# A two-layer encoder on one core: softmax divided on ScalarE, layer norms ended in halves, and a smaller DMA scratch traded for four buffers

## Chip, core and metric

The kernel runs on one core of a Trainium2 chip. The metric is the time of one execution on the device in microseconds (us), the median of the runs shown. Engines are named as in the profile: PE (TensorE's matmuls), PEld (its weight loads), DVE (VectorE), ACT (ScalarE), POOL (GpSimd) and SP (SyncE, which only issues DMAs).

## The reference

The input x has 512 tokens of 1024 numbers, the memory 256 tokens. Two layers follow each other, each with four blocks that end in a layer norm:

```python
for i in range(DEPTH):                                   # DEPTH = 2
    y = swiglu(x, ffn_w_gate[i, 0], ffn_w_up[i, 0], ffn_w_down[i, 0])
    x = layer_norm(ALPHA * x + 0.5 * y, ln_g[i, 0], ln_b[i, 0])
    if i % 2 == 0:
        y = mixer_ab(x, ...)      # 8 heads of dense attention, 8 heads within a window of 128
    else:
        y = mixer_c(x, ...)       # 16 heads, each token sees its neighbours on a grid
    x = layer_norm(ALPHA * x + y, ln_g[i, 1], ln_b[i, 1])
    y = memory_attn(x, mem, ...)  # 4 heads into the 256 memory tokens
    x = layer_norm(ALPHA * x + y, ln_g[i, 2], ln_b[i, 2])
    y = swiglu(x, ffn_w_gate[i, 1], ffn_w_up[i, 1], ffn_w_down[i, 1])
    x = layer_norm(ALPHA * x + 0.5 * y, ln_g[i, 3], ln_b[i, 3])
```

`layer_norm` is `(x - mu) * rsqrt(var + eps) * g + b` over the 1024 numbers of a token. Each attention takes a softmax, `exp(s - m) / sum(exp(s - m))`, over the scores of a query.

## The kernel before

All is in float32, and products keep nearly all its digits: `split` (line 360) writes each operand as a high part, rounded on ACT, and a low part, the difference taken on DVE, and `mm3` multiplies three times. So every weight and every intermediate result passes ACT and DVE on its way to PE. The residual x stays in SBUF as four blocks of 128 tokens, `x[t]`; `xh` and `xl` are its two parts with the features on the partitions, made by transposes on PE (`to_features`). The steps of a layer stand in `run`: FFN, mixer, memory attention, FFN.

**Softmax.** In all four attentions a block of queries has its scores in a PSUM bank. DVE takes the extreme score, ACT the exponential and its sum `l` over the row, DVE the reciprocal of `l`, and then `normalise` multiplies the row by it, in place, in an SBUF tile of the tag "t2" (shown as `t` in the profile, as `t_643` and the like in an order). After that PE transposes the row, ACT and DVE split the transposed bank, and PE multiplies with the values. `normalise` chooses the engine by an argument: DVE for the first block of four in dense attention, for blocks 0 and 3 in the neighbourhood attention (whose row it writes as pieces of 64), and for the first of each pair in memory attention; POOL for all others, and for all of windowed attention. In all there are 160 such multiplications: 32 of 512 columns (dense), 16 of 384 and 16 of 256 (windowed), 32 of 192 and 32 of 256 (neighbourhood), 32 of 256 (memory). Dense and windowed attention keep two heads ahead of the one that is being transposed.

**Layer norm.** `layer_norm(t, ...)` follows the last product of block t: DVE makes `nmu` (minus the mean) and `(x + nmu) * g` into a slab, ACT the sum of squares (tile `junk`), POOL the inverse root (`lny`) in two small instructions, and DVE writes `x[t]` with one last instruction of 1024 columns. Only the very last block of the kernel does that in two halves, with an output DMA behind each. `to_features` then transposes the block eight times, four of them from each half of the columns.

**Memory.** SBUF tiles rotate: 27 of the tag "slab" (4 KB per partition) and 14 of "t2" (2 KB per partition). A scratch at the bottom of SBUF, left at its default size, serves the DMAs that POOL issues (line 1628 makes the program). Those are the additions of weight quarters onto slabs by DMA, the gains and offsets of the norms, the additions of x, and the bias tables.

**Order.** No instruction goes out where it is written. `Graph.record` (line 136) notes each with a price in ns by `cost`, `plan` (line 179) lays all of them out on five engines, one instruction at a time, with the buffers as they come free, `deadlines` gives each a due time, and a second plan by due times fixes the order of every engine. The kernel then issues in that order. The price takes in that DVE and POOL can hold each other up: an instruction whose `op.port` is set waits in the plan for the other engine's last one that has it. Since every call goes out from line 154, groups in the profile are told apart by their tiles.

Of the kernel before, what the change touches and what calls it, by code (L numbers as in the profile page):

```python
# [65 lines left out]
class Graph:  # L66
# [69 lines left out]
    def record(self, engine, method, args, kw):  # L136
        kw = dict(kw)
        aps = [z for z in list(args) + list(kw.values()) if hasattr(z, "tensor")]
        outs = [kw[k] for k in ("out", "accum_out") if k in kw]
        if "out" not in kw:  # L140
            outs.insert(0, args[0])
        ins = [z for z in aps if not any(z is o for o in outs)]
        op = Op()
        op.engine, op.index, op.dma, op.adds = engine, len(self.ops), method == "dma_start", "accum_op" in kw
        op.rank = op.index
        op.ns = self.cost(engine, method, outs[0], ins, kw)
        func = args[2] if method == "activation" else None
        op.table = str(func) if func in (AF.Silu, AF.Exp) else None
        op.size = math.prod(outs[0].shape) * 4
        op.port = method in ("tensor_tensor", "scalar_tensor_tensor", "tensor_scalar") and (  # L150
            engine == "gpsimd" or engine == "vector" and op.ns > 250.0 and all(z.space != bass.MemoryType.PSUM for z in ins)
        )
        fn = getattr(getattr(self.nc, engine), method)
        op.call = lambda: fn(*args, **kw)  # L154
        op.deps, op.users, op.frees, op.later = set(), [], [], []
        if self.after and engine in self.after[1]:
            op.deps.add(self.after[0])
        for z, writes in [(z, False) for z in ins] + [(z, True) for z in outs]:
            info = self.tiles.get(z.tensor.name)
            if info is None:  # L160
                continue
            p0, p1, runs = self.extent(z)
            opens = writes and kw.get("start", False)
            keep = []
            for q, w, a0, a1, other in info["log"]:
                over = opens or p0 < a1 and a0 < p1 and (
                    info["bank"] and q.engine != engine or any(l < b and a < h for l, h in runs for a, b in other)
                )
# [148 lines left out]
class Kernel:  # L317
# [16 lines left out]
        return f"{s}_{self.n}"  # L334


    BUFS = {"t2": 14, "slab": 27, "raw": 2, "a": 3, "d": 2, "t": 3}

    def tile(self, pool, shape, dt, tag, bufs=None):
        return self.nc.tile(pool, shape, dt, tag, self.name(tag), bufs or self.BUFS.get(tag, 1))  # L340
# [134 lines left out]
    def layer_norm(self, t, st, gb, last):  # L475

        nc = self.nc
        g, b = gb[:2]
        x = self.x[t]
        halves = [(0, 512), (512, D)] if last and t == NT - 1 else [(0, D)]  # L480
        nmu = self.small(1, "nmu", 4)
        nc.vector.tensor_scalar(nmu, st[:, 0:1], st[:, 1:2], -1.0 / D, ALU.add, ALU.mult)
        var = self.small(1, "var", 4)
        if len(gb) < 3:
            gb.append([])
        if len(gb[2]) < 2:
            gb[2].append(self.slab(F32))
        y = gb[2][t % 2]
        nc.vector.scalar_tensor_tensor(out=y, in0=x, scalar=nmu, in1=g, op0=ALU.add, op1=ALU.mult)
        nc.scalar.activation(self.junk, x, AF.Square, bias=nmu, scale=1.0, accum_out=var)  # L490
        r = self.rsqrt(var, 1, "ln", 1.0 / D, LN_EPS / ALPHA**2)
        for lo, hi in halves:
            nc.vector.scalar_tensor_tensor(
                out=x[:, lo:hi], in0=y[:, lo:hi], scalar=r, in1=b[:, lo:hi], op0=ALU.mult, op1=ALU.add
            )
            if last:
                dst = self.out.rearrange("(r c) d -> c r d", c=GRID_W)[16 * t : 16 * t + 16, :, lo:hi]
                nc.sync.dma_start(out=dst, in_=x[:, lo:hi])
# [421 lines left out]
        self.split(ps[:, lo:hi], h[:, lo:hi], l[:, lo:hi], scale)  # L920
        return h, l

    def normalise(self, u, r, on_vector):
        if not on_vector:
            self.nc.gpsimd.tensor_tensor(out=u, in0=u, in1=r.broadcast_to(list(u.shape)), op=ALU.mult)
        elif u.shape[1] % 192 == 0:

            self.nc.vector.tensor_scalar(u.rearrange("p (z n) -> p z n", n=64), u, r, None, ALU.mult)
        else:
            self.nc.vector.tensor_scalar(u, u, r, None, ALU.mult)  # L930

    def softmax(self, u, rows, mn, lo, n, sums=None, on_vector=False):

        nc = self.nc
        l = self.small(1, "l")
        nc.scalar.activation(u[:rows, :n], sums if sums is not None else u[:rows, :n], AF.Exp, bias=mn[:rows], scale=-1.0, accum_out=l[:rows])
        nc.vector.reciprocal(l[:rows], l[:rows])
        self.normalise(u[:rows, lo:n], l[:rows], on_vector)


    def rope(self, src, n_heads, tab, t, dst):
# [42 lines left out]
    def mixer_ab(self, ln_i, last):  # L984
        nc, a = self.nc, self.a
# [81 lines left out]
        for cg, t in ((1, 0), (1, 1), (1, 2), (0, 0), (1, 3), (0, 1), (0, 2), (0, 3)):  # L1067
            ps = proj(self.ps("a"), t, w1 if cg else w0)
# [16 lines left out]
        def weights_a(pr, s):  # L1085

            p, q = {}, made[False, pr]
            for t in range(NT):
                ps = scores(q[s], kA[s], t, 0, S)
                mn = self.small(1, "mn")  # L1090
                nc.vector.tensor_reduce(out=mn, in_=ps, axis=AX.X, op=ALU.min)
                u = self.t2(F32)
                self.softmax(u, P, mn, 0, S, sums=ps, on_vector=t == 0)
                for kk in range(NT):
                    p[t, kk] = u[:, kk * P : (kk + 1) * P]
            return p
# [73 lines left out]
        for n in range(8):  # L1170
            h, t = divmod(n, 4)
# [8 lines left out]
        for n, (f, v, pr, s) in enumerate(heads):  # L1180
# [39 lines left out]
    def mixer_c(self, ln_i, last):  # L1220
        nc, a = self.nc, self.a
# [74 lines left out]
        def weights_of(pair):  # L1296

            got = []
            for q, k, table in zip(qs.pop(pair), ks.pop(pair), biases(pair)):
# [3 lines left out]
                l = self.small(4, "l4")  # L1303
                us = []
                for t, (kc, w, kind) in enumerate(C_BLOCKS):
                    n = w * ROWS
# [12 lines left out]
                    us.append(u)  # L1319
                nc.vector.reciprocal(l, l)  # L1320
                for t, u in enumerate(us):
                    self.normalise(u, l[:, t : t + 1], t in (0, 3))
                got.append([z[:, c * 256 : c * 256 + 256] for z in both for c in range(2)])
            return got

# [84 lines left out]
    def memory(self, i, ln_i, last):  # L1410
# [36 lines left out]
        def weights_of(kt, q):  # L1447
            p = []
            for tt in range(2):
# [13 lines left out]
                u = self.t2(F32)  # L1463
                for j in range(2):
                    c = slice(j * 256, j * 256 + 256)
                    self.softmax(u[:, c], P, mn[:, j : j + 1], 0, 256, sums=ps[:, c], on_vector=j == 0)
                p.append(u)
            return p

# [165 lines left out]
```

## Time and profile before

| | |
|---|---|
| median of 3 runs | 2139.68 us (2139.59 to 2140.12) |
| the profiled execution's own time | 2138.68 us |
| its span in the profile | 2136.9 us |
| granted clock of PE, mean | 0.998 |
| PE busy | 2114.8 us of the span |
| DVE, ACT, POOL busy | 1764.7, 1081.7 and 379.9 us |

The two attentions of the first mixer lie between 392 and 530 us of the span, dense before 463 and windowed after it; the neighbourhood attention lies between about 1400 and 1620 us. PE's busy time is the union of its matmuls, which overlap, so short waits don't show in it; the idle times of PEld, with what ended them, show more of these. A mean duration is that of one instruction from its start to its end; on one engine, the end of one can lie behind the start of the next.

### The profile page before, as it was taken

Reading aid. Unit: us, or ns where it says so; the run is one execution under the profiler, and the core shown is the slowest. Engines: PE = TensorE matmul, PEld = TensorE weight load, DVE = VectorE, ACT = ScalarE, POOL = GpSimd, SP = SyncE. Lnnn points to the kernel's source line nnn. Section 1 sums busy time; section 2 is a strip of 40 time slices with the busy share of each in tenths; the row PEclk is TensorE's granted clock in tenths of the full one; section 3 lists DMA queues with packets and bytes.
Section 4 is the critical chain, followed back from the end, with each engine's and each line's share of the span. In section 5 each row is a group of like instructions: output and inputs, shape, how many; then the busy total and the mean of one; then the engine's idle time right before and its main releaser. Section 6 shows DMA issues by size and latency. Waiting matters only on the chain.

```text
span 2136.9 us, 33147 instructions
## 1 busy us (share of the span) xinstructions
PE 2114.8 (99%) x12904; PEld 1885.1 (88%) x12904; DVE 1764.7 (83%) x2501; ACT 1081.7 (51%) x1703; POOL 379.9 (18%) x483
## 2 busy tenths in 40 slices
PE   9999999999999999999999999999999999999997
PEld 7999988778888899999889999888888888999996
DVE  7789988898748969999879999876677479699996
ACT  5555543576435544545545455445554355444552
POOL 0001015544002100000200000414420021000003
PEclk9999999999999999999999999999999999999999
DMA  6566562003443246655445556355454432456551
GB/s 206 144 160 147 138 186 88 20 21 97 141 138 99 89 109 188 158 148 138 136 101 130 141 137 180 90 158 147 134 153 156 139 97 91 109 148 157 140 147 60
DMA packets 208717, 275.95 MB, mean 129 GB/s; under 512 B 10673, under 2 KB 151601, under 8 KB 208561
## 3 DMA queue, kind: packets, MB, share of 16 engines
q1 hardware_dynamic: 175760, 221.14, 33.1%
q0 software_dynamic: 32512, 52.44, 13.7%
q8 instruction: 102, 1.67, 0.3%
q14 instruction: 55, 0.44, 0.1%
q10 hardware_dynamic: 288, 0.26, 0.0%
HBM read 259.12 MB, written 4.19 MB: 123 GB/s over the span
## 4 chain that ended last, share of the span: by engine, by line
PE 95%; DVE 3%; ACT 1%; issue 1%; DMA 0%; POOL 0%; POOLq 0%; DVEq 0%; SPq 0%; ACTq 0%
PE a L154 58%; PE d L154 22%; PE t L154 15%; DVE slab L154 1%; DVE x L154 1%; ACT slab L154 1%; DVE t L154 0%; ACT t L154 0%; DMA slab<-t 0%; DMA raw<-x_t 0%; DVE mn L154 0%; POOL t L154 0%; DVE xl L154 0%; POOLq L1631 0%; ACT xh L154 0%
## 5 line engine op out<-in xcount | busy, mean ns | idle before, releaser
L154 DVE TENSOR_TENSOR slab<-slab,slab 128x1024 fp32r<-128x1024 f32 (+3 forms) x638 | 729.3, 1168 | 72.6 <-ACT slab L154 33.1
L154 ACT CAST slab<-slab 128x1024 fp32r<-128x1024 f32 (+2 forms) x498 | 472.4, 983 | 338.6 <-DVE slab L154 139.0
L154 PE MATMUL a<-slab,slab 128*128 128x256 f32 (+2 forms) x2456 | 566.3, 314 | 0.8 <-ACT t L154 0.5
L154 PE MATMUL a<-xh,slab 128*128 128x256 f32 (+2 forms) x2480 | 559.5, 315 | 0.3 <-ACT slab L154 0.3
L154 PE MATMUL d<-slab,slab 128*128 128x512 f32 (+2 forms) x1856 | 449.7, 382 | 2.3 <-DVE x L154 1.8
L154 PEld LDWEIGHTS a<-slab,slab 128*128 128x128 f32 x2456 | 416.5, 190 | 34.7 <-ACT t L154 3.0
L154 PEld LDWEIGHTS a<-xh,slab 128*128 128x128 f32 x2480 | 416.1, 190 | 33.9 <-ACT slab L154 1.0
L154 PE MATMUL a<-xl,slab 128*128 128x256 f32 (+1 forms) x1240 | 389.7, 314 | 0.0
L154 PE MATMUL a<-raw,slab 128*128 128x256 f32 x2048 | 388.7, 283 | 0.9 <-DVE t L154 0.9
L154 PEld LDWEIGHTS d<-slab,slab 128*128 128x128 f32 x1856 | 328.4, 189 | 61.0 <-DVE x L154 2.9
L154 PEld LDWEIGHTS a<-raw,slab 128*128 128x128 f32 x2048 | 327.8, 192 | 6.1 <-ACT slab L154 1.3
L154 PEld LDWEIGHTS a<-xl,slab 128*128 128x128 f32 x1240 | 236.1, 190 | 18.1
L154 PE MATMUL t<-slab,slab 128*128 128x512 f32 (+1 forms) x864 | 209.2, 383 | 0.0
L154 DVE TENSOR_TENSOR slab<-raw,slab 128x1024 fp32r<-128x1024 f32 (+2 forms) x132 | 163.9, 1255 | 19.2 <-ACT slab L154 19.1
L154 PEld LDWEIGHTS t<-slab,slab 128*128 128x128 f32 x864 | 151.4, 189 | 25.1
L154 ACT CAST slab<-t 128x512 fp32r<-128x512 f32 (+2 forms) x211 | 114.1, 567 | 72.0 <-PE t L154 39.0
L154 DVE TENSOR_TENSOR slab<-t,slab 128x512 fp32r<-128x512 f32 (+2 forms) x211 | 132.2, 646 | 10.0 <-ACT slab L154 9.0
L154 ACT CAST slab<-raw 128x1024 fp32r<-128x1024 f32 (+1 forms) x124 | 123.0, 1022 | 28.3 <-PE a L154 9.0
L154 DVE SCALAR_TENSOR_TENSOR x<-d,x 128x512 f32<-128x512 f32 x168 | 114.9, 686 | 17.7 <-PE d L154 16.9
L154 POOL TENSOR_TENSOR t<-t,l 128x256 f32<-128x256 f32 (+2 forms) x104 | 82.9, 819 | 258.8 <-DVE l L154 257.9
L154 ACT COPY t<-a 128x512 f32<-128x512 f32 x96 | 56.3, 587 | 123.7 <-PE a L154 70.1
L154 POOL DMA_DIRECT2D slab<-ffn_w_down x40 | 47.8, 1194 | 313.1 <-DVE slab L154 294.6
(127 smaller groups left out, 2182.5 us busy)
## 6 DMA issues: line engine op xcount, KB each, us to landing
slab<-ffn_w_gate SPq DMA_DIRECT2D x80, 512.0 KB
slab<-ffn_w_up SPq DMA_DIRECT2D x80, 512.0 KB
slab<-ffn_w_down SPq DMA_DIRECT2D x80, 512.0 KB
slab<-ffn_w_down POOLq DMA_DIRECT2D x40, 512.0 KB, 5.6
raw<-mem_w_kv SPq DMA_DIRECT2D x16, 1024.0 KB
slab<-t SPq DMA_DIRECT2D x96, 128.0 KB
slab<-ffn_w_gate POOLq DMA_DIRECT2D x16, 512.0 KB, 7.7
slab<-ffn_w_up POOLq DMA_DIRECT2D x16, 512.0 KB, 5.8
```

Source lines behind the costliest of these rows:

```text
L154: op.call = lambda: fn(*args, **kw)
```

## The change

It has four parts. `normalise` always runs on ACT, as an activation that copies the row with the reciprocal as its scale. `layer_norm` ends in two instructions of 512 columns for blocks 2 and 3 of every norm (for block 2 of the last norm with two output DMAs in place of one). The program is made with 4096 bytes of DMA scratch, and there are 29 slabs and 16 t2 tiles in place of 27 and 14. And in the prices, `op.port` of a DVE instruction asks for 64 columns or more in place of a price over 250 ns.

```diff
-            engine == "gpsimd" or engine == "vector" and op.ns > 250.0 and all(z.space != bass.MemoryType.PSUM for z in ins)
+            engine == "gpsimd" or engine == "vector" and math.prod(outs[0].shape[1:]) >= 64 and all(z.space != bass.MemoryType.PSUM for z in ins)
...
-    BUFS = {"t2": 14, "slab": 27, "raw": 2, "a": 3, "d": 2, "t": 3}
+    BUFS = {"t2": 16, "slab": 29, "raw": 2, "a": 3, "d": 2, "t": 3}
...
-        halves = [(0, 512), (512, D)] if last and t == NT - 1 else [(0, D)]
+        halves = [(0, 512), (512, D)] if t > 1 else [(0, D)]
...
-    def normalise(self, u, r, on_vector):
-        if not on_vector:
-            self.nc.gpsimd.tensor_tensor(out=u, in0=u, in1=r.broadcast_to(list(u.shape)), op=ALU.mult)
-        elif u.shape[1] % 192 == 0:
-
-            self.nc.vector.tensor_scalar(u.rearrange("p (z n) -> p z n", n=64), u, r, None, ALU.mult)
-        else:
-            self.nc.vector.tensor_scalar(u, u, r, None, ALU.mult)
-
-    def softmax(self, u, rows, mn, lo, n, sums=None, on_vector=False):
+    def normalise(self, u, r):
+        self.nc.scalar.activation(u, u, AF.Copy, scale=r)
+
+    def softmax(self, u, rows, mn, lo, n, sums=None):
...
-        self.normalise(u[:rows, lo:n], l[:rows], on_vector)
+        self.normalise(u[:rows, lo:n], l[:rows])
...
-    nc = bacc.Bacc("TRN2", target_bir_lowering=False, num_devices=1)
+    nc = bacc.Bacc("TRN2", target_bir_lowering=False, num_devices=1, dynamic_dma_scratch_size=4096)
```

(The three callers of `softmax` and `normalise` drop the argument that chose the engine.)

The plan changes with it. On ACT, this is the start of dense attention before, just behind the load of the exponential's table; rows that write `t` and `l` are exponentials with their sums, those from `t` to `slab` are halves of queries:

```order
L154 ACTIVATE t_643_724,l_725<-a_722,mn_723 128x512
L154 ACTIVATE slab_642<-t_699 64x128
L154 ACTIVATE t_647_728,l_729<-a_726,mn_727 128x512
L154 ACTIVATE t_655_736,l_737<-a_734,mn_735 128x512
L154 ACTIVATE slab_642<-t_706 64x128 x2
L154 ACTIVATE slab_751<-t_750 64x512
L154 ACTIVATE t_651_732,l_733<-a_730,mn_731 128x512
L154 ACTIVATE t_659_740,l_741<-a_738,mn_739 128x512
```

And the same place after; rows that read and write one `t` tile, with an `l`, are the divisions:

```order
L154 ACTIVATE t_643_724,l_725<-a_722,mn_723 128x512
L154 ACTIVATE t_639_720<-t_639_720,l_721 128x512
L154 ACTIVATE slab_642<-t_699 64x128
L154 ACTIVATE t_647_728,l_729<-a_726,mn_727 128x512
L154 ACTIVATE t_655_736,l_737<-a_734,mn_735 128x512
L154 ACTIVATE slab_642<-t_706 64x128
L154 ACTIVATE t_643_724<-t_643_724,l_725 128x512
L154 ACTIVATE t_647_728<-t_647_728,l_729 128x512
L154 ACTIVATE slab_642<-t_706 64x128
L154 ACTIVATE t_659_740,l_741<-a_738,mn_739 128x512
L154 ACTIVATE t_651_732,l_733<-a_730,mn_731 128x512
```

The divisions stand between the exponentials, two to six rows behind the one that they belong to; whatever follows a division waits behind it on the same engine.

On DVE, at the norm ahead of the neighbourhood attention, block 2 (`x_6`) before; `st` are the sums for the mean, `xl` the low parts of transposed blocks:

```order
L154 SCALAR_TENSOR_TENSOR slab_2500<-x_6_87,nmu_2521,slab_2493 128x1024
L154 SCALAR_TENSOR_TENSOR x_7_88,st_2526<-d_2527,x_7_88 128x512
L154 SCALAR_TENSOR_TENSOR x_7_88,st_2526<-a_2528,x_7_88 128x512
L154 SCALAR_TENSOR_TENSOR x_6_87<-slab_2500,lny_2523,slab_2494 128x1024
L154 TENSOR_SCALAR nmu_2529<-st_2526 128x1
```

And after:

```order
L154 SCALAR_TENSOR_TENSOR slab_2500<-x_6_87,nmu_2521,slab_2493 128x1024
L154 TENSOR_TENSOR xl_84<-t_2512,xh_83 128x4x128
L154 SCALAR_TENSOR_TENSOR x_7_88,st_2526<-d_2527,x_7_88 128x512
L154 SCALAR_TENSOR_TENSOR x_6_87<-slab_2500,lny_2523,slab_2494 128x512
L154 SCALAR_TENSOR_TENSOR x_7_88,st_2526<-a_2528,x_7_88 128x512
L154 SCALAR_TENSOR_TENSOR x_6_87<-slab_2500,lny_2523,slab_2494 128x512
L154 TENSOR_SCALAR nmu_2529<-st_2526 128x1
```

The first half of block 2 is written one instruction of block 3 earlier, the second half behind that instruction.

On PE, at the same norm, the transposes of block 2 (`ident` and `x_6`) before, between products of the next stage:

```order
L154 MATMUL a_2543<-slab_2539,xh_83 128x256
L154 MATMUL t_2524<-ident_78,x_6_87 128x128 x4
L154 MATMUL t_2525<-ident_78,x_6_87 128x128 x4
L154 MATMUL a_2543<-slab_2540,xh_83 128x256
L154 MATMUL a_2543<-slab_2539,xl_84 128x256
```

And after:

```order
L154 MATMUL a_2543<-slab_2539,xl_84 128x256
L154 MATMUL t_2524<-ident_78,x_6_87 128x128 x4
L154 MATMUL a_2544<-slab_2537,xh_83 128x256
L154 MATMUL a_2544<-slab_2538,xh_83 128x256
L154 MATMUL t_2525<-ident_78,x_6_87 128x128 x4
```

The eight transposes that stood together are two groups of four with two products between them, and the first now stands behind the last product of `a_2543`.

More of the change, by code (lines that the diff above doesn't have):

```diff
@@ L1092, in weights_a @@
                 u = self.t2(F32)
-                self.softmax(u, P, mn, 0, S, sums=ps, on_vector=t == 0)
+                self.softmax(u, P, mn, 0, S, sums=ps)
                 for kk in range(NT):
@@ L1321, in weights_of @@
                 for t, u in enumerate(us):
-                    self.normalise(u, l[:, t : t + 1], t in (0, 3))
+                    self.normalise(u, l[:, t : t + 1])
                 got.append([z[:, c * 256 : c * 256 + 256] for z in both for c in range(2)])
@@ L1465, in weights_of @@
                     c = slice(j * 256, j * 256 + 256)
-                    self.softmax(u[:, c], P, mn[:, j : j + 1], 0, 256, sums=ps[:, c], on_vector=j == 0)
+                    self.softmax(u[:, c], P, mn[:, j : j + 1], 0, 256, sums=ps[:, c])
                 p.append(u)
```

## Prediction

> **What bounds the kernel now.** First the head of the page and of its chain.
>
> ```profile
> span 2136.9 us, 33147 instructions
> PE 2114.8 (99%) x12904; PEld 1885.1 (88%) x12904; DVE 1764.7 (83%) x2501; ACT 1081.7 (51%) x1703; POOL 379.9 (18%) x483
> PE 95%; DVE 3%; ACT 1%; issue 1%; DMA 0%; POOL 0%; POOLq 0%; DVEq 0%; SPq 0%; ACTq 0%
> ```
>
> TensorE is busy 99% and carries 95% of the chain. The change takes no matmul away, so it can only win time in which TensorE waits. That time is small: 2136.9 - 2114.8 = 22.1 us by the busy time, with the start and the end of the program in it. Next the stretches of the mixers: dense attention (A, 392 to 463), windowed attention (B, to 530), neighbourhood attention (C, 1400 to 1620).
>
> ```profile
> core 0: us, PE busy (x) PEld busy (x) DVE busy (x) ACT busy (x) POOL busy (x), PEclk, DMA share, GB/s
> 392.00:463.00 71.00, 68.66 (x360) 54.96 (x358) 65.34 (x141) 47.13 (x112) 36.76 (x41) 1.00 0.06 16
> 463.00:530.00 67.00, 64.76 (x394) 56.84 (x393) 59.85 (x166) 48.37 (x127) 32.90 (x64) 1.00 0.23 64
> 1400.00:1620.00 220.00, 219.81 (x1380) 196.26 (x1380) 155.61 (x332) 115.91 (x260) 66.47 (x122) 1.00 0.54 156
> ```
>
> In A and B together TensorE is busy 133.42 of 138 us, VectorE 125.19 (91%), ScalarE 95.50 (69%). In C TensorE misses 0.2 us of 220, so C has nothing to give. Matmuls overlap and hide short waits in the busy time, so I take the waits of the weight loads, in the stretch of A and B:
>
> ```profile
> PEld t L154 <- DVE slab L154: 4.5, 9, 1.8
> PEld a L154 <- ACT t L154: 3.0, 9, 0.7
> PEld d L154 <- DVE x L154: 1.4, 2, 0.9
> PEld t L154 <- PE a L154: 0.6, 1, 0.6
> PEld d L154 <- ACT slab L154: 0.5, 1, 0.5
> PEld a L154 <- DVE slab L154: 0.5, 1, 0.5
> PEld d L154 <- ACT t L154: 0.4, 1, 0.4
> PEld d L154 <- DVE slab L154: 0.3, 1, 0.3
> ```
>
> Sum 11.2 us, more than a third of the kernel's waits. VectorE ends 4.5 + 1.4 + 0.5 + 0.3 = 6.7 of it (it empties PSUM banks late), ScalarE 3.9. POOL is not in the list: its divisions are waited for only indirectly.
>
> **The change, part by part.**
>
> *The division.* These rows, in order, are the divisions of today (first three POOL, next three VectorE) and ScalarE's nearest operations, with a pointer operand and SBUF on both sides:
>
> ```profile
> L154 POOL TENSOR_TENSOR t<-t,l 128x256 f32<-128x256 f32 x64 | 40.7, 650 | 217.4 <-DVE l L154 217.1
> L154 POOL TENSOR_TENSOR t<-t,l 128x512 f32<-128x512 f32 x24 | 27.5, 1167 | 24.9 <-DVE l L154 24.9
> L154 POOL TENSOR_TENSOR t<-t,l 128x384 f32<-128x384 f32 x16 | 15.5, 974 | 16.5 <-DVE l L154 15.9 <-ACT slab L154 0.5
> L154 DVE TENSOR_SCALAR t<-t,l 128x192 f32<-128x192 f32 x32 | 19.7, 646 | 0.4
> L154 DVE TENSOR_SCALAR t<-t,l 128x512 f32<-128x512 f32 x8 | 10.5, 1312 | 0.0
> L154 DVE TENSOR_SCALAR t<-t,l 128x256 f32<-128x256 f32 x16 | 8.8, 570 | 0.2
> L154 ACT ACTIVATE t<-t,mn 128x385 f32<-128x385 f32 x16 | 9.8, 616 | 4.1 <-DVE mn L154 4.1
> L154 ACT ACTIVATE t<-t,mn 128x257 f32<-128x257 f32 x16 | 8.1, 508 | 0.7 <-POOL t L154 0.3 <-DVE mn L154 0.2
> L154 ACT ACTIVATE t<-t,mn 128x192 f32<-128x192 f32 x32 | 14.2, 445 | 4.6 <-issue 3.8 <-DVE mn L154 0.5
> L154 ACT ACTIVATE junk<-x,nmu 128x1024 bf16<-128x1024 f32 x32 | 36.8, 1151 | 66.6 <-DVE nmu L154 61.9 <-issue 4.7
> ```
>
> 104 divisions leave POOL, 56 VectorE (39.0 us), and 160 come to ScalarE. By these widths a ScalarE division of 512 is between 616 (385 wide) and 1151 (1024 wide): on the line, 722 ns; 384 wide 616, 256 wide 508, 192 wide 445. When operations stand back to back, each takes about 0.1 less:
>
> ```profile
> 333.02 1.07 ACT L154 CAST xh<-t 128x512 fp32r<-128x512 f32 x2 [0.88 <-PE t L154]
> L154 ACT CAST xh<-t 128x512 fp32r<-128x512 f32 x56 | 30.7, 587 | 48.8 <-PE t L154 48.8
> ```
>
> (two of 587 in 1.07 us). A and B have 32 of 512, 16 of 384, 16 of 256: 23.1 + 9.9 + 8.1 = 41.1 us alone, 41.1 - 6.4 = 34.7 back to back. ScalarE then has 95.5 + 34.7 = 130.2 to 136.6 us of work in a stretch that takes 138 and in which TensorE needs 138 - 11.2 = 126.8. VectorE falls by the 10.5 us of its eight 512-wide divisions to 114.7. So the fullest helper changes from VectorE at 91% to ScalarE. By these figures the stretch could shrink by at most 138 - 130.2 = 7.8 us. ScalarE's 95.5 hold many operations that stand alone and would close up, so 130.2 is rather too much.
>
> In its favour: VectorE's division is irregular where POOL works beside it, and the plan that fixes all orders prices it at 399 ns (512 / 1.92 + 132), against 1312 measured.
>
> ```profile
> L154 DVE TENSOR_SCALAR t<-t,l x8: 486/1241/2684, 395.0 to 462.7; 128x512 f32<-128x512 f32 x8
> ```
>
> The same formulas price ScalarE's at 572, some 50 ns under my back-to-back 622. The written order will lie closer to what happens, and the nine waits on "DVE slab" are of the sort that such surprises make. I take 5.0 of the 6.7 us as gone and 1.0 more on ScalarE: **-4.0 us**, between -7.8 and +9 (below). What is late next is ScalarE: exponentials and first halves of the splits stand behind a division that waits for its reciprocal. In C the 64 divisions are 32 x 0.445 + 32 x 0.508 = 30.5 us beside 115.9 of 220; with that room they cost nothing. In memory attention 16 per layer, 8.1 us, lie likewise; 0.
>
> [...]
>
> *The halves.* Two norms are followed by a visible wait of TensorE's transposes, at 341 to 350 us (first row) and at 1390 to 1402 (the next):
>
> ```profile
> PEld t L154 <- issue: 0.9, 1, 0.9
> PEld t L154 <- issue: 1.0, 1, 1.0
> L154 DVE SCALAR_TENSOR_TENSOR x<-slab,lny,slab 128x1024 f32<-128x1024 f32 x31 | 39.6, 1280 | 1.0 <-POOL lny L154 0.9
> L154 DVE SCALAR_TENSOR_TENSOR x<-slab,lny,slab 128x512 f32<-128x512 f32 x2 | 1.4, 747 | 0.4 <-POOL lny L154 0.4
> ```
>
> The first four transposes may go 1280 - 747 = 533 ns earlier: 2 x 0.53 = **-1.1 us**; from 0 to the whole 1.9. Fifteen norms gain an instruction, each 1.4 - 1.28 = 0.12 us, 1.8 us in all on VectorE, mostly beside matmuls. At the very end block 2's two halves keep the last norm's POOL power where it is, or let it in between them (-0.6 to +0.1): 0.
>
> *Buffers, scratch, prices.* The ring of POOL's DMAs shrinks to a quarter.
>
> ```profile
> q0 software_dynamic: 32512, 52.44, 13.7%
> ```
>
> 32512 packets over 112 issues are 290 each, some 18 per engine. No row shows what the ring can hold; what hides a delay is that the added quarters are wanted a whole step of matmuls later. I take 0, between 0 and +6 (each of the 112 late by 50 ns on the path). The four buffers and the new order elsewhere: TensorE already runs without gaps through the FFNs, so at best the stray waits go, such as this at 128 us:
>
> ```profile
> PEld a L154 <- ACT slab L154: 1.3, 1, 1.3
> ```
>
> I take **-0.9**, from -4 to +4, since a new order can also open waits of this size.
>
> Sum: -4.0 - 1.1 - 0.9 = **-6.0 us**. Against the profiled execution (2138.68, its span of 2136.9 and 1.8 around it) that is 2132.7; the median of the runs is 2139.68, 1.0 above it, so I forecast **2133.7**.
>
> **Rivals.**
> 1. *ScalarE becomes the queue of A and B* (slower). Its place is the heads between 392 and 530. If ScalarE can be filled no better than VectorE is today (125.19 of 138, 90.7%), its middle of 133.4 us needs 147: +9, less 2 from the other parts, 2146.7. It decides from where ScalarE's need passes TensorE's 126.8 us, which by its busy time it does. Against it: ScalarE's isolated operations close up, and VectorE and POOL get room.
> 2. *Waits change their name.* As many waits go from "DVE slab" as come on "ACT"; only the halves stay: -1.1, 2138.6. For it: ScalarE ends 3.9 us of the waits already at 69%.
> 3. *The change doesn't do what it says*: the plan shifts waits elsewhere or the small ring delays POOL's DMAs: +6, 2145.7. Against it: the gapless FFNs and the 18 packets.
>
> **Chances.** My forecast, with larger gains, 0.50; the second rival and what lies near it 0.27; the first 0.17; the third 0.06. A measurement of this kernel tells about 0.2% (4.3 us) from no change: faster 0.50, same 0.27, slower 0.23. The range runs from 2125 (7.8 + 1.9 + 4, and about 1 of the rest) to 2145, just short of the first rival's middle, so that about a tenth lies beyond each end.
>
> **What would show it.** Right: waits of the weight loads on "DVE slab" between 390 and 530 fall below 2 us, and that stretch is some 4 us shorter, with ScalarE over 92% busy; the two norms' waits halve. Wrong: rows "PEld t" or "PEld a" ended by ACT sum to over 8 us there (first rival), or to as much as VectorE loses (second); gaps in the FFNs, or "POOL DMA" rows far over their present durations (third). A ScalarE division of 512 well over 722 ns would break the sum.

## The result, and the profile after

The changed kernel takes **2144.69 us** (2142.46 to 2147.01, 11 runs) beside 2140.02 of the kernel before (2138.16 to 2141.77, 11 runs): ratio 1.0022, 95% interval 1.0015 to 1.003. It is slower by 4.7 us, little but clear of 1 by its interval, where 6 us less was forecast.

The head and the chain of waits of the profile after:

```profile
span 2142.3 us, 33001 instructions
PE 2117.1 (99%) x12904; PEld 1885.7 (88%) x12904; DVE 1725.2 (81%) x2460; ACT 1151.2 (54%) x1863; POOL 288.0 (13%) x379
PE 91%; ACT 3%; DMA 3%; DVE 2%; issue 1%; POOL 0%; SPq 0%; DVEq 0%; ACTq 0%
```

VectorE and POOL lost 39.5 and 92 us of work, ScalarE took 69.5 more, as the change says. But TensorE's share of the chain fell from 95 to 91%, and DMA, at 0% before, has 3%. The same three stretches as in the prediction, with their columns:

```profile
core 0: us, PE busy (x) PEld busy (x) DVE busy (x) ACT busy (x) POOL busy (x), PEclk, DMA share, GB/s
392.00:463.00 71.00, 69.48 (x370) 55.90 (x369) 58.21 (x138) 65.36 (x145) 11.57 (x21) 1.00 0.06 16
463.00:530.00 67.00, 66.10 (x393) 57.04 (x391) 56.11 (x161) 61.92 (x159) 5.02 (x27) 1.00 0.26 70
1400.00:1620.00 220.00, 212.97 (x1321) 188.29 (x1320) 127.13 (x289) 136.53 (x319) 34.59 (x86) 0.99 0.55 152
```

In the first two TensorE is busier than before (135.6 of 138 us in place of 133.4). In the third, where it had missed 0.2 us of 220, it now misses 7.0. What it waits for there is in the waits of the weight loads from 1400 to 1625 us; first before, then after (total, times, longest):

```profile
PEld t L154 <- DVE t L154: 1.7, 6, 0.3
PEld a L154 <- DMA slab<-t: 0.4, 1, 0.4
```

```profile
PEld a L154 <- DMA slab<-t: 5.1, 2, 4.5
PEld a L154 <- issue: 2.9, 3, 1.8
PEld t L154 <- DVE t L154: 2.1, 6, 0.4
```

`slab<-t` are the copies that `queries` and `keys` of the neighbourhood attention end with: twelve of 128 KB per pair of heads, four from `queries` and eight from `keys`, issued by SP, from which the scores of a later pair are made. The 4.5 us are one wait, for the eight of the last pair's keys. On the timeline around it (start, duration, and in brackets the idle time and what ended it), before:

```profile
1572.82 4.97 SPq L154 DMA_DIRECT2D slab<-t  x8
1580.65 0.57 POOL L154 DMA_DIRECT2D slab<-ln_g  x1 [12.19 <-DVE mn L154]
1584.13 1.20 POOL L154 TENSOR_TENSOR t<-t,l 128x256 f32<-128x256 f32 x2 [2.92 <-DVE l L154]
...
1586.76 0.59 POOL L154 DMA_DIRECT2D slab<-ln_b  x1
```

and after:

```profile
1572.35 0.56 POOL L154 DMA_DIRECT2D slab<-ln_g  x1 [14.79 <-PE t L154]
1572.91 0.54 POOL L154 DMA_DIRECT2D slab<-ln_b  x1
1573.01 5.41 SPq L154 DMA_DIRECT2D slab<-t  x8
1583.79 0.33 PE L154 MATMUL a<-slab,slab 128*128 128x192 f32 x1 [4.10 <-DMA slab<-t]
1584.56 0.73 PE L154 MATMUL a<-slab,slab 128*128 128x192 f32 x3 [0.45 <-DMA slab<-t]
```

SP issues the copies at nearly the same time in both. The norm's gains and offsets (`ln_g`, `ln_b`, 512 KB each on POOL's queue, which VectorE first needs for the norm at 1610 us) went out 8 and 14 us after the first copy; now they go out just ahead of it. What the queues then move from 1575 to 1578 us (packets, MB, share of the 16 engines), after:

```profile
q0 software_dynamic: 109, 0.42, 91.7%
q1 hardware_dynamic: 3, 0.00, 0.4%
```

and before:

```profile
q1 hardware_dynamic: 403, 0.66, 89.0%
```

q0 is POOL's queue, q1 SP's. For three microseconds POOL's queue holds the engines nearly alone, and the copies, of which five more are issued in these 3 us, stand still. The 0.42 MB are less than the 512 KB of one load, so the first load, of the gains, is enough for that; in the microsecond behind it POOL's queue still has 87.3% and SP's 10.6%.

To compare stages of kernels that run at different times, I count TensorE's waiting at equal points of its work: the start of each matmul, less the sum of the usual pitches of all matmuls ahead of it (0.227 us for 512 columns, 0.120 for 256, the medians in the kernel before). Its growth by stage in us (worked out from the starts of all 12904 matmuls of each profile; the experiments are those below):

| stage | before | after | e3 | e6 | e8 | e9 | e12 |
|---|---|---|---|---|---|---|---|
| to the first mixer | 5.6 | 4.6 | 4.5 | 3.8 | 6.1 | 3.4 | 3.5 |
| dense and windowed attention | 10.9 | 9.2 | 9.3 | 9.1 | 9.4 | 8.3 | 8.2 |
| then to the second mixer's norm | 3.9 | 4.5 | 4.1 | 3.9 | 3.2 | 4.6 | 3.0 |
| that norm | 2.2 | 1.8 | 1.8 | 2.8 | 2.2 | 2.8 | 2.8 |
| neighbourhood attention | 5.6 | 15.3 | 9.3 | 6.4 | 11.3 | 15.9 | 6.7 |
| the rest | 2.5 | 1.6 | 1.6 | 2.8 | 1.5 | 2.0 | 2.1 |
| sum | 30.6 | 37.0 | 30.6 | 28.8 | 33.6 | 36.9 | 26.1 |

One profile is one execution: that of e5, which has the orders of the kernel before on every engine and differs by its scratch alone, sums to 32.2 in place of 30.6, so I read nothing into differences of 1.6 us between two profiles unless runs or several profiles agree.

The changed kernel was 2.5 us ahead when it came to the neighbourhood attention, and lost 9.7 there. By the same count 5.0 of these (4.3 and 0.7) are the wait at 1579 us; a second, of 1.7 and 0.5 us at 1486 us, is also for copies. And right behind the long wait the granted clock of TensorE (the column PEclk) is at half for 3.4 us, and then at full again (columns as above):

```profile
1584.90:1588.30 3.40, 3.40 (x19) 3.40 (x18) 1.87 (x10) 2.19 (x8) 0.00 (x0) 0.50 1.01 363
1588.30:1592.00 3.70, 3.70 (x24) 3.33 (x24) 1.32 (x9) 2.94 (x11) 0.00 (x0) 1.00 0.42 168
```

Half of 3.4 us makes 1.7 us more, as an estimate. That makes 8.9 of the 9.7 us; the rest is spread over the stage. The kernel before has no such stretch until its matmuls are over.

### The profile page after: what moved, and what is told of

It reads as the page before. It is cut to its first block, busy times and chain, and to the rows that moved or that the text cites. A ratio compares the mean times of both kernels' runs of the same rounds, so it can differ in the third digit from the quotient of the medians.

```text
span 2142.3 us, 33001 instructions
## 1 busy us (share of the span) xinstructions
PE 2117.1 (99%) x12904; PEld 1885.7 (88%) x12904; DVE 1725.2 (81%) x2460; ACT 1151.2 (54%) x1863; POOL 288.0 (13%) x379
## 4 chain that ended last, share of the span: by engine, by line
PE 91%; ACT 3%; DMA 3%; DVE 2%; issue 1%; POOL 0%; SPq 0%; DVEq 0%; ACTq 0%
PE a L154 57%; PE d L154 20%; PE t L154 14%; ACT t L154 2%; ACT slab L154 1%; DVE slab L154 1%; DMA slab<-t 1%; DMA slab<-ffn_w_up 1%; DVE t L154 0%; DVE x L154 0%; DMA raw<-ab_w_out 0%; DMA raw<-c_w_in 0%; DMA raw<-x_t 0%; DMA raw<-mem_t 0%; DVE mn L154 0%
## 5 line engine op out<-in xcount | busy, mean ns | idle before, releaser
L154 PE MATMUL a<-slab,xh 128*128 128x512 f32 (+1 forms) x272 | 79.5, 375 | 0.8 <-ACT xh L154 0.7
```

## The experiments

Three theories stood at the start. **Theory 1**: a POOL without divisions issues its loads earlier, and they run into the copies. **Theory 2**: ScalarE's queue delays the parts of the queries and keys. **Theory 3**: the four new buffers free the loads' slabs earlier. Ratios are to the kernel before, on the same chip, with 95% intervals; each profile is of one execution.

### e1: the old divisions, everywhere

The changed kernel, with `normalise` and its callers as before; halves, buffers, scratch and prices stay.

```diff
-    def normalise(self, u, r):
-        self.nc.scalar.activation(u, u, AF.Copy, scale=r)
+    def normalise(self, u, r, on_vector=None):
```

> The changed kernel with the softmax divided on VectorE and POOL as before; halves, price rule, small scratch and the four buffers stay. Theory 1 (freed POOL): the neighbourhood attention lost about 10 us because POOL, rid of its divisions, issues its DMAs (gains and offsets of the norm, bias tables) earlier, into the copies of queries and keys that TensorE waits for; with the divisions back the 10 us go and about 2.5 us of the gain in the first mixer go too: about 2137 us. Theory 2 (ScalarE queue in the neighbourhood attention): the same 2137. Theory 3 (buffers): the slabs of these loads come free earlier because there are 29, so the collision stays: 2145 to 2147 us.

Measured: 2141.67 us, ratio 1.0005 (0.9996 to 1.0013): between the theories. The gains still go out early, at 1572.16 us, but the offsets at 1585.69, behind the last divisions, and the wait is 0.75 us instead of 4.3 and 0.7, with no stretch at half clock. So the gains go early whoever divides; that the offsets follow at once comes from the divisions' leaving POOL.

### e2: the old buffers

The changed kernel with the buffers and the scratch of before.

```diff
-    BUFS = {"t2": 16, "slab": 29, "raw": 2, "a": 3, "d": 2, "t": 3}
+    BUFS = {"t2": 14, "slab": 27, "raw": 2, "a": 3, "d": 2, "t": 3}
-    nc = bacc.Bacc("TRN2", target_bir_lowering=False, num_devices=1, dynamic_dma_scratch_size=4096)
+    nc = bacc.Bacc("TRN2", target_bir_lowering=False, num_devices=1)
```

> The changed kernel with 27 slabs, 14 t2 tiles and the default DMA scratch; divisions on ScalarE, halves and the price rule stay. Theory 1 (freed POOL): the collision stays, some wait of TensorE on the copies of queries of over 3 us near the end of the neighbourhood attention, 2143 to 2147 us. Theory 3 (buffers): it goes, 2138 to 2140 us. Theory 2 (ScalarE queue): stays, but with waits that ScalarE ends.

Measured: 2140.07 us, 0.9998 (0.999 to 1.0007). POOL's rows on the timeline:

```profile
1584.17 0.56 POOL L154 DMA_DIRECT2D slab<-ln_g  x1 [19.88 <-DVE mn L154]
1584.84 0.54 POOL L154 DMA_DIRECT2D slab<-ln_b  x1
```

With 27 slabs POOL waits 12 us longer for a slab, and both loads go out behind the copies; no wait is left at 1579 us. Theories 1 and 3 are each half right: the buffers make the slab free early, and the empty POOL lets the second load follow. Waits of 1.7 and 1.1 us at 1486 to 1490 us stay, here with a stretch at half clock behind them, so these do not hang on the buffers.

### e3: the norm's loads behind the copies

The changed kernel; in `mixer_c` the two loads are issued by SP.

```diff
-    def load_ln(self, i):
+    def load_ln(self, i, queue="gpsimd"):
...
-            self.nc.gpsimd.dma_start(out=z, in_=self.a[name][i : i + 1, :].broadcast_to([P, D]))
+            getattr(self.nc, queue).dma_start(out=z, in_=self.a[name][i : i + 1, :].broadcast_to([P, D]))
...
-        gb = self.load_ln(ln_i)
+        gb = self.load_ln(ln_i, "sync")
```

> The changed kernel, with the two loads of gains and offsets of the norm behind the neighbourhood attention issued by SP in place of POOL; there they stand behind the copies of queries and keys. Theory 1 and theory 3 (a collision of these loads with the copies): the wait of 4.1 us and the 0.5 behind it go, 2144.7 - 4.6 = about 2140 us; the waits at 1486 us (2.2) stay. Theory 2 (ScalarE queue): no change, 2144 to 2145 us.

Measured: 2138.53 us, 0.9992 (0.9983 to 1.0001), against 1.0022 of the changed kernel. The loads now go out behind the copies on the same queue:

```profile
1572.86 5.07 SPq L154 DMA_DIRECT2D slab<-t  x8
1579.82 0.64 PE L154 MATMUL d<-slab,slab 128*128 128x256 f32 x4
1580.02 0.42 SPq L154 DMA_DIRECT2D slab<-ln_g  x1
1580.53 0.59 SPq L154 DMA_DIRECT2D slab<-ln_b  x1
```

TensorE goes on without a wait, and the granted clock stays at 1.00. The part of the stage with this wait falls from 7.3 to 1.1 us, the time by 6.2. Theory 2's "no change" is out for this wait. Only the queue of these two loads was changed (and what the plan made of it), so the wait at 1579 us is shown to be the collision with them.

### e4: the old divisions in the neighbourhood attention alone

The changed kernel; POOL and VectorE divide in the neighbourhood attention as before.

```diff
-                    self.normalise(u, l[:, t : t + 1])
+                    self.normalise(u, l[:, t : t + 1], t in (0, 3))
```

> The changed kernel, with the old division on VectorE and POOL in the neighbourhood attention alone (dense, windowed and memory attention divide on ScalarE). Theories 1 and 2: the gain of the first mixer and the norms (3.8 us up to 770 us) stays and the 10 us of the neighbourhood attention go: 2135 to 2138 us. Theory 3 (buffers): 2142 us or more, since the loads still find a slab early.

Measured: 2138.66 us, 0.9991 (0.9982 to 1.0). Gains at 1571.76 us, offsets at 1585.01, a wait of 0.83 us. The same reading as from the first run, though the time is 0.7 us above the range of theories 1 and 2. It is also 3.0 us below the first run, which differs only in that VectorE and POOL divide in the other attentions too.

### e5: each part alone: the scratch

Here and in e6 to e10 the base is the kernel before.

```diff
-    nc = bacc.Bacc("TRN2", target_bir_lowering=False, num_devices=1)
+    nc = bacc.Bacc("TRN2", target_bir_lowering=False, num_devices=1, dynamic_dma_scratch_size=4096)
```

> The kernel before with nothing but the 4 KB of DMA scratch. Collision theory (the early loads of the last norm's gains and offsets delay the copies of the last pair): the scratch sets no order, so no change, ratio 0.999 to 1.001 (2138 to 2142 us), and the additions of ffn_w_down take 5.5 to 6 us from issue to landing, as before. Rival (the small ring delays POOL's DMAs): 3 us or more slower, 2143 us or above, with longer times from issue to landing.

Measured: 2140.1 us, 1.0004 (0.9995 to 1.0013): no effect that can be told. POOL's additions of `ffn_w_down`, 512 KB each, land 5.7 us after their issue (median of 40), against 5.6 before.

### e6: each part alone: the buffers (with the scratch that pays for them)

```diff
-    BUFS = {"t2": 14, "slab": 27, "raw": 2, "a": 3, "d": 2, "t": 3}
+    BUFS = {"t2": 16, "slab": 29, "raw": 2, "a": 3, "d": 2, "t": 3}
```

> The kernel before with 29 large and 16 small buffers and the 4 KB of scratch; divisions, norms and prices as before. Collision theory in its two-condition form (the load needs an early slab, and the offsets need a POOL free of divisions): the gains go out near 1572 us instead of 1580, the offsets stay behind the four divisions, and the wait near 1579 us is under 1.2 us; 2139 to 2142 us. Rival (the buffers alone cause the loss): a wait of over 4 us near 1579 us and 2143 to 2146 us.

Measured: 2137.21 us, 0.999 (0.9981 to 0.9998): better than either theory had it.

```profile
1568.51 0.58 POOL L154 DMA_DIRECT2D slab<-ln_g  x1 [7.39 <-PE t L154]
1576.26 0.62 PE L154 MATMUL a<-slab,slab 128*128 128x192 f32 x3 [0.41 <-DMA slab<-t]
1581.54 0.60 POOL L154 DMA_DIRECT2D slab<-ln_b  x1
```

The gains are early and TensorE waits 0.4 us, and 0.3 more at 1578 us; the offsets are held back by the divisions at 1580.4. Elsewhere the buffers win: 1.8 us ahead of the first mixer and 1.8 in its two attentions.

### e7: each part alone: the halves

```diff
-        halves = [(0, 512), (512, D)] if last and t == NT - 1 else [(0, D)]
+        halves = [(0, 512), (512, D)] if t > 1 else [(0, D)]
```

> The kernel before with nothing but the halves of the layer norms. If the gain ahead of the first mixer is theirs: TensorE's wait at 341 to 350 us falls from 1.75 to under 0.5, other norms gain up to 0.5 each, the stage of the neighbourhood attention stays at 5 to 6 us of waits; 2136.5 to 2139 us, ratio 0.9985 to 0.9995. Rival (the added instructions on VectorE cost what they win, or the plan shifts other waits in): 2139.5 to 2142 us.

Measured: 2137.98 us, 0.9991 (0.9983 to 1.0), within the expected range, but not by its reasons. The first norm's wait falls from 1.75 to 0.61 us and 1.1 of new waiting comes right behind it; the second norm's stays (2.21, then 2.23); others gain nothing. The profiled execution is only 0.5 us shorter (span 2136.4). What it wins lies at the very end: from the last matmul to the end of the span 11.5 us instead of 12.3.

### e8: each part alone: the divisions

```diff
-    def normalise(self, u, r, on_vector):
+    def normalise(self, u, r):
+        self.nc.scalar.activation(u, u, AF.Copy, scale=r)
```

> The kernel before with nothing but ScalarE's divisions; buffers, scratch, norms and prices as before. Collision theory: without the four buffers the gains go out after 1580 us, no wait of over 1.2 us near 1579, and TensorE's waits in the two first attentions fall from 10.9 to 9 to 10 us; 2138 to 2141 us. Rival (ScalarE's queue costs in the neighbourhood attention whatever the buffers are): waits there rise from 5.5 to over 12 us and the time is 2144 us or more.

Measured: 2141.77 us, 1.0007 (0.9998 to 1.0015), 0.8 above the expected range and 2.2 below the rival's. Waits in the two first attentions are 9.4 us, as expected, and there is none at 1579 us. But the neighbourhood attention rises from 5.6 to 11.3 us of waiting, by waits for copies of 2.0 us at 1487 and others near 1490 and 1536, and by 3.4 us at half clock from 1491.1 us on. The rival asked for over 12, so it nearly holds for the waits: divisions on ScalarE cost in that stage even without the new buffers. By which step, the queue of ScalarE or the new order, this run does not tell.

### e9: buffers and divisions together

Both edits above, with norms and prices as before.

> The kernel before with ScalarE's divisions and with 29 large and 16 small buffers (and the 4 KB of scratch); norms and prices as before. These two alone measured 2137.2 us (buffers) and 2141.8 (divisions) beside 2139.6 of before. Theory of two conditions (the four buffers free the slabs early, the empty POOL lets the offsets follow the gains at once): TensorE waits over 3.5 us near 1579 us, though neither part alone had 1.2 us there, and the time is 2143 to 2147 us. Rival (the parts add up, the long wait hangs on the halves or the prices): no wait over 1.5 us there, 2138 to 2140.5 us.

Measured: 2142.76 us, 1.0014 (1.0005 to 1.0023). The time is 0.2 below the expected range, and the wait is 2.2 and 0.7 us in place of "over 3.5"; the rival's "no wait over 1.5" is out.

```profile
1573.71 0.56 POOL L154 DMA_DIRECT2D slab<-ln_g  x1 [14.79 <-PE t L154]
1574.27 0.54 POOL L154 DMA_DIRECT2D slab<-ln_b  x1
1574.37 5.38 SPq L154 DMA_DIRECT2D slab<-t  x8
1583.24 0.33 PE L154 MATMUL a<-slab,slab 128*128 128x192 f32 x1 [2.20 <-DMA slab<-t]
```

Both loads go out just ahead of the copies, as in the changed kernel. Neither part alone does this; halves and prices aren't needed for it. The wait is shorter than in the changed kernel, but not by a later TensorE: loads, copies and TensorE all come 1.4 us later, after 3.2 us lost at 1485. What differs is that the loads went faster. This is POOL's queue from 1572 to 1585 us (packets, MB, share of the engines), after and in this run:

```profile
q0 software_dynamic: 288, 1.05, 36.7%
```

```profile
q0 software_dynamic: 288, 1.05, 29.4%
```

The offsets landed 8.6 us after their issue instead of 10.6; why, no run shows. The stage loses as much as in the changed kernel all the same (15.9 us), since here the clock is at half for 3.4 us twice, behind the wait at 1485 and behind this one.

### e10: buffers and halves together

The edits of e6 and e7, with divisions and prices as before.

> The kernel before with the four buffers, the scratch and the halves; divisions and prices as before (with the new price rule the same measured 2141.7 us). If these two parts add up: 2135 to 2136.5 us, ratio 0.998 to 0.9985, and the new price rule costs some 5 us by the order that it sets. Rival (the halves and the buffers do not add up, the rule is nothing): 2140 to 2143 us, with the wait of 1.9 us at 1488 us.

Measured: 2139.48 us, 0.9996 (0.9987 to 1.0005), with no wait at 1488 us. The runs fall between the two theories, while the profiled execution (span 2135.3) would fit the first: the runs' median lies 4.2 us above the span here, -0.5 to 3.3 in the other kernels. Whether the two parts add up stays open; the wait at 1488 does not come from them.

### e11: old divisions in the neighbourhood attention and the loads on SP

The edits of e3 and e4 on the changed kernel.

> The changed kernel with the old divisions in the neighbourhood attention alone and, there, the loads of the norm's gains and offsets issued by SP behind the copies. Each of the two alone measured 2138.6 us beside 2140.3 of before. If both act on the one collision: no more than 1.5 us below either, 2137 to 2138.7 us, no wait over 0.6 us near 1579, the wait of 1.7 us at 1488 us stays. Rival (they act on different waits and add up): 2132 to 2135 us.

Measured: 2137.34 us, 0.9989 (0.998 to 0.9998). The long wait is gone, and hardly more is gained than by either edit alone, as expected if both act on the one collision. But 0.7 us of waiting for copies are left at 1582 us, just over the expected 0.6, though the loads go out behind the copies (1581.3 us), and the wait at 1486 us did not stay at 1.7 but grew to 2.6, with a stretch at half clock behind it: TensorE comes 0.4 us earlier than in e4, and the copies that it waits for land 0.5 us later.

### e12: buffers, and divisions outside the neighbourhood attention

The kernel before with 29 slabs, 16 t2 tiles and the scratch, and this; `mixer_c` still calls `normalise` with `t in (0, 3)`.

```diff
-    def normalise(self, u, r, on_vector):
-        if not on_vector:
+    def normalise(self, u, r, on_vector=None):
+        if on_vector is None:
+            self.nc.scalar.activation(u, u, AF.Copy, scale=r)
+        elif not on_vector:
...
-                self.softmax(u, P, mn, 0, S, sums=ps, on_vector=t == 0)
+                self.softmax(u, P, mn, 0, S, sums=ps)
```

> The kernel before with the four buffers and the scratch, and ScalarE's divisions in dense, windowed and memory attention alone; norms, prices and neighbourhood attention as before. If the divisions win in the first two attentions what the waits say (about 1.5 us) and the order elsewhere stays as with the buffers alone: 2135 to 2136.5 us. Rival (the new order shifts waits of 1 to 2 us in, as the new prices did): 2137.5 to 2141 us.

Measured: **2135.42 us**, 0.998 (0.9971 to 0.999): below both kernels. Its three stretches:

```profile
392.00:463.00 71.00, 70.31 (x374) 56.73 (x373) 59.86 (x141) 65.94 (x145) 10.75 (x23) 1.00 0.06 16
463.00:530.00 67.00, 65.48 (x387) 55.97 (x387) 56.18 (x158) 60.32 (x155) 4.63 (x23) 1.00 0.29 79
1400.00:1620.00 220.00, 219.06 (x1359) 194.07 (x1358) 153.36 (x332) 115.36 (x260) 55.52 (x117) 1.00 0.54 152
```

The first two are as full as in the changed kernel (135.8 us), and TensorE misses 0.9 us in the third instead of 7.0. Against the buffers alone (e6) the waiting in the first two falls from 9.1 to 8.2 us, where 1.5 was expected, and the intervals of the two times overlap.

### e13: the second wait: a third load buffer

The wait at 1485 to 1488 us divides the kernels in two. Behind the 1 MB loads of `c_w_in`, SP issues the copies of a pair; the distance from the first of these loads to the first copy, and TensorE's waits for the copies from 1482 to 1494 us, both read from the timelines and waits:

| kernels | distance, us | waits, us |
|---|---|---|
| e6, e10, e12, later e14 | 6.7 to 6.8 | none |
| before, e5, e7 | 5.2 to 5.5 | 0.2 to 0.3 |
| after, e1, e2, e3, e4, e8, e9, e11 | 2.8 to 3.4 | 1.9 to 3.0 |

The changed kernel with one load buffer more and two slabs less.

```diff
-    BUFS = {"t2": 16, "slab": 29, "raw": 2, "a": 3, "d": 2, "t": 3}
+    BUFS = {"t2": 16, "slab": 27, "raw": 3, "a": 3, "d": 2, "t": 3}
```

> The changed kernel with a third load buffer (raw 3 in place of 2) paid for by two slabs (27 in place of 29); all else as changed. If the wait at 1485 to 1488 us comes from the 1 MB loads of c_w_in that go out just ahead of the copies: the loads go out 5 us or more ahead of the copies and the wait falls from 2 us to under 0.6. With 27 slabs the gains of the last norm go out after 1580 us, so the 4.3 us near 1579 go too. Together 2136 to 2139 us. Rival (the copies are late by their own source, whatever goes before): the wait there stays at 1.5 us or more, 2138.5 to 2141 us.

Measured: 2136.38 us, 0.9982 (0.9973 to 0.9991). The long wait is gone, as with any 27 slabs (gains at 1579.46 us). But the loads go out only 2.2 us ahead of the copies, so the third buffer did not do what it was for, and the wait of 1.5 us stays. This run therefore does not tell whether the distance is the cause.

### e14: the second wait: the old prices

The kernel of e4, with the old price rule.

```diff
-            engine == "gpsimd" or engine == "vector" and math.prod(outs[0].shape[1:]) >= 64 and all(z.space != bass.MemoryType.PSUM for z in ins)
+            engine == "gpsimd" or engine == "vector" and op.ns > 250.0 and all(z.space != bass.MemoryType.PSUM for z in ins)
```

> The changed kernel with the old divisions in the neighbourhood attention and the old price rule (so e4_neighbourhood_as_before, which measured 2138.7 us, without the new prices). If the new prices open the wait at 1488 us by the order of the casts of c_w_in: the loads go out over 5 us ahead of the copies, the wait is under 0.6 us, 2135 to 2137 us. Rival (the halves together with the buffers do it): the wait stays at 1.5 us or more and 2138 to 2140 us.

Measured: 2137.35 us, 0.9987 (0.9979 to 0.9996), a little above the expected range. SP's timeline with the new prices (e4), then with the old:

```profile
1476.27 1.51 SPq L154 DMA_DIRECT2D raw<-c_w_in  x2
1479.44 7.86 SPq L154 DMA_DIRECT2D slab<-t  x8
```

```profile
1472.50 3.90 SPq L154 DMA_DIRECT2D raw<-c_w_in  x2
1479.23 5.45 SPq L154 DMA_DIRECT2D slab<-t  x8
```

One line of prices moves the loads by 3.8 us, and the wait goes with it. Some of what that frees is lost at 1577 us, where TensorE now waits 1.8 us for copies behind the early gains, instead of 0.8. In both kernels the gains go out 0.6 us ahead of the first copy, so why the wait is longer stays open; one early load alone is not always cheap. So the new prices open the second wait, and so do ScalarE's divisions in this stage (e8, which has the old prices). That the distance of loads and copies makes the wait fits all sixteen kernels, but no run changed the distance alone.

## Why the prediction was wrong

**The step that failed** is "so C has nothing to give", with the zero for its 64 divisions ("with that room they cost nothing"). The idle 0.2 us said that there was nothing to win; I read it as nothing to lose. The stage lost 9.7 us. ScalarE's room (115.9 of 220 us, now 136.5) was not the limit that matters. What matters is the order in which transfers go out: POOL's divisions were a gate in POOL's queue, which held the 512 KB of offsets back until the copies had landed, and the shortage of slabs was another for the gains. The change opened both. Behind the wait that followed the clock was at half for 3.4 us, a price that no term of the sum had.

**The buffers, scratch and prices, -0.9 from -4 to +4.** The scratch was rightly 0. The buffers alone won 2.1 us by the ratio (e6). What I did not ask is which transfer an earlier free slab would start, and into what. Together with the divisions, that is the wait shown above; e3 prices it at 6.2 us, outside my +4.

**The third rival had the number.** Its 2145.7 us lie 1.0 from the measured time, and its words "the plan shifts waits elsewhere" fit; it had a chance of 0.06. That the number is so near is luck: its +6 was worked out from 112 late DMAs of the small ring. The evidence set against it, the gapless FFNs and the 18 packets, speaks of the small scratch and of another stage. The two loads that matter were not delayed; they were too early.

**Dense and windowed attention, -4.0.** Sign right, size not: the waiting there falls by 1.7 us in the changed kernel, and by 1.5 with the divisions alone. The prices of the step hold. ScalarE's divisions, after:

```profile
L154 ACT ACTIVATE t<-t,l 128x256 f32<-128x256 f32 x80 | 36.2, 503 | 0.9 <-DVE l L154 0.9
L154 ACT ACTIVATE t<-t,l 128x512 f32<-128x512 f32 x32 | 21.6, 735 | 0.0
L154 ACT ACTIVATE t<-t,l 128x192 f32<-128x192 f32 x32 | 14.2, 447 | 1.0 <-DVE l L154 0.9
```

735 ns for 512 columns against 722 estimated; ScalarE has 127.3 of 138 us (92.2%) against "over 92%", VectorE 114.3 against 114.7. What failed is "I take 5.0 of the 6.7 us as gone". The waits of the weight loads from 392 to 530 us, after:

```profile
PEld t L154 <- DVE slab L154: 5.6, 11, 1.0
PEld a L154 <- ACT t L154: 1.7, 5, 0.5
PEld t L154 <- ACT t L154: 0.7, 3, 0.3
```

The waits on "DVE slab" rose from 4.5 to 5.6 us instead of falling below 2, though the slow divisions have left VectorE (the longest fell from 1.8 to 1.0). So the divisions did not make most of them. Those on ScalarE fell from 3.9 to 2.4 us, though ScalarE is fuller by 31.8 us: the first rival, which made ScalarE the queue of these stages, is wrong in its place.

Nor is the gain of 1.7 us shown to be the divisions' work. The first run (e1) has the other three parts and the old divisions, and TensorE is as busy there (columns as in the stretches above):

```profile
392.00:463.00 71.00, 69.99 (x370) 56.07 (x369) 63.89 (x143) 49.21 (x116) 38.55 (x44) 1.00 0.06 16
463.00:530.00 67.00, 65.31 (x394) 57.36 (x393) 57.22 (x163) 47.84 (x124) 31.35 (x60) 1.00 0.29 76
```

That is 135.3 of 138 us, against 135.6 in the changed kernel; the halves alone (e7) have 134.8, the buffers alone 134.3, the divisions alone 135.2, the kernel before 133.4. Each of these parts sets a new order, and each new order is better here, so the right sign is in part luck. The times say that ScalarE's divisions outside the neighbourhood attention gain something (e4 is 3.0 us below e1, e12 1.8 below e6, by the medians), but where, no run shows.

The price of a division doesn't speak against ScalarE: the waits in these two attentions fell, and a division of 512 columns took 735 ns on ScalarE against 1312 on VectorE. Of VectorE's eight before, the one with no multiplication of POOL beside it took 486 ns; the others, each with one or two beside it, took 1069 to 2684.

**The halves, -1.1.** The first norm's wait went from 1.75 to 0.17 us, but it also goes without halves (0.07 in e6, 0.05 in e9), and 0.9 comes back right behind it. The second norm's fell by 0.4. The end of the program, put at 0 between -0.6 and +0.1, won some 0.9 us, from the start of the last matmul to the end of the span (11.2 to 11.7 in the ten profiles with halves, 12.0 to 12.5 in the six without, the kernel before among them). POOL's last instruction there, the second `lny` of the last block, takes 0.94 us in each of the ten and 1.47 in each of the six; that makes about half of the gain.

**The sum of the parts.** By the ratios, the buffers give -2.1 us, the halves -1.9, the divisions +1.5; the prices some +1 to +2 (e4 against e14, e1 against e10, each within its uncertainty). That would be about -1; measured was +4.7. The difference is as large as what e3 wins back from the collision (6.2), which no part makes by itself. But the parts do not add up elsewhere either: buffers and halves together gave -0.9 (e10), where their sum is -4.0.

## What to carry to other kernels

A stage without idle time has nothing to give and everything to lose: ask there, too, which transfer an emptier engine or one more buffer will start, and what stands on the DMA engines at that moment. Work on an engine that also issues DMAs can be the only thing that keeps a big, early load behind a small, urgent one (with the same buffers the offsets went out at 1585.69 us behind POOL's divisions, e1, and at 1572.91 without them); if that work moves, put the order down by hand, for example by issuing the load on the queue of the urgent one, behind it. Test the parts of a change alone and in pairs: here no part that ran alone lay above the kernel before by more than its interval, and the pair of buffers and divisions did. And before a gain is put down to a part, look at the same stage in a run without that part: where every order is planned anew, any part can shift the waits.

## What the runs showed of the hardware

**A load ahead of copies.** With two loads of 512 KB on it, POOL's queue took 91.7% of the DMA engines' time for 3 us and left SP's queue 3 packets, while several copies of 128 KB were waiting on it. The two loads have 288 packets on POOL's queue, of which 109 fall in these 3 us. By what rule the engines choose between the two queues, and why POOL's, by then with the offsets (0.42 MB in the 3 us and 0.34 in the next are more than one load), still had 87.3% of the next microsecond, no run shows. The rate in the 3 us is low as well: 0.42 MB, 141 GB/s, against 0.66 MB before. The gains' load landed 6.7 us after its issue and the offsets' 10.6, against 4.0 for the gains before:

```profile
slab<-ln_g POOLq DMA_DIRECT2D x1, 512.0 KB, 6.7
slab<-ln_b POOLq DMA_DIRECT2D x1, 512.0 KB, 10.6
```

**A long wait and the clock.** In the neighbourhood attention the granted clock fell to 0.50 for 3.4 us once each in the changed kernel, e2, e8 and e11 and twice in e9, each time within 1.5 us behind waits of TensorE that sum to 2.3 us or more (4.6 in the changed kernel; 2.5, 2.3 and 2.6; 3.0 and 2.9). Behind waits of up to 2.1 us (e3, at 1486 us) it stayed at 1.00, and the other ten profiles have no such stretch in this stage. In it the ten matmuls that take 1.28 us in e3 (from 1579.82 us) took 2.13 in the changed kernel (from 1585.09 us).
